# A hybrid decoder trunk: stick-breaking values scaled inside the attention's first unit, the gate block's subtractions side by side, the first group's transposes one step later, one quick pair fewer

## The chip, the core and the metric

The kernel runs on one core of a Trainium2 chip. The core has five engines that work side by side, each through its own queue in order: TensorE (PE in the profile, with its weight loads as PEld), VectorE (DVE), ScalarE (ACT), GpSimd (POOL) and SyncE (SP), which issues the DMAs. The metric is the time of one launch on the device, in microseconds (us); lower is better.

## The reference

Two layers work on 256 tokens of width 2048, all in float32. Each layer is:

```python
h = rms_norm(x, attn_norm)
g_q, g_k, g_v, g_gate, g_lr, s_q, s_k, s_v = split(h @ w_in)
log_a = log_sigmoid(g_lr @ w_gate_up + b_gate) / 16
o_gla = rms_norm(gla_chunked(g_q, g_k, g_v, log_a)) * silu(g_gate)   # 8 heads, chunks of 64
o_sb  = rms_norm(stick_breaking(rms_norm(s_q), rms_norm(s_k), s_v))  # 8 heads of 128
x = x + concat(o_gla, o_sb) @ w_o
x = x + square(relu(rms_norm(x, mlp_norm) @ w_up)) @ w_down          # 8192 hidden
```

Inside a chunk the gated linear attention works with `exp(b)`, `exp(-b)` and `exp(b_end - b)`, where `b` is the running sum of `log_a`. The stick-breaking attention weighs a key by `exp(log sigmoid(z) + suffix)`, where `suffix` is the sum of `log sigmoid(-z)` over the later keys before the query. It is computed as a product with a triangular matrix.

## The kernel before

**Products in parts.** The float32 operands of a large product are split into a high part, in a format that PE takes in one pass, and a low part, the rest; a product is three matmuls (high x high, high x low, low x high). The activations are split once. The weights are split while they stream in: SP loads a raw tile, ACT copies it into a high part `whi`, DVE subtracts to give the low part `wlo`. So every weight costs PE, ACT and DVE time, and the three engines work in a pipeline.

**Two ways to order the work.** Most of the time lies in `listed()`. It writes down all pieces of a long stretch (PE products in a fixed order, ACT and DVE pieces with lengths and dependences) and lets `Plan.run()` order ACT and DVE by due times, counted backwards from the PE pieces that need them. A first list (`front`) makes the three head blocks of layer 0: stick-breaking keys "sk", values "sv" and gated values "gv". A second one, per layer, makes the gate block, the output projection, the MLP and the three head blocks of the next layer. Each block goes over eight pairs of 128-row tiles. A pair in the table `QUICK` (or `FAST`, `QUICK_OUT`) is done in seven products of half-size blocks in place of eight, at the price of sums on DVE (line 821) and four weight parts in place of two. Lines 984 and 988 make the parts here, line 1078 is the matmul. The weight parts go round a ring of `RING = 5` slots: slot 0 is the list's own, slots 1 to 4 are the four `whi`/`wlo` tiles that are shared with the stretch in between.

**The attention stretch** lies between the lists and is written as a plain program, which the framework then orders by when it thinks things are ready. It is a chain of units of PE work:

- `ua`: the gate's low-rank columns and a quarter of the stick-breaking queries (272 columns, 8 steps). Lines 592 and 593 make its parts, 609, 612 and 615 are its matmuls.
- `ub`: the next quarter of the queries (256 columns, 8 steps).
- `uq`: the second half of the queries (512 columns, 8 steps).
- four units of `unit_t` (4 steps each, lines 634 and 638): the gated queries and keys.

After each step `tick()` is called. Other work hangs on the steps: `after(n, fn)` runs `fn` n steps later, and its ACT and DVE instructions queue behind the newest weight part on these engines. `sb_heads` does a group of four stick-breaking heads in two pairs: scores (`sb_scores`), three steps later the weights (`sb_weights`, whose exponentials are lines 757 and 758), one step later the outputs and their norm, and `last` steps later `to_operand`, which transposes the result on PE (line 788) and splits it (lines 793 and 794). `sb_qk` scales and norms the queries (lines 659 to 664) and turns them on PE (line 699). `gates(b)`, twice per layer, makes the three exponentials for the gated keys and queries. `row_of` spreads the row of inverse norms by two transposes (line 569) of a tile that POOL writes (line 568). Small PE results go through four PSUM banks in turn (`ps_tile`), so a tile waits for the readers of the fourth tile before it.

**The values.** `vs["sv", c]` holds half of the stick-breaking values, unscaled. `values()` multiplies them by the tokens' inverse norm on ACT (line 800, four instructions per layer) into tiles `v4`. In the kernel before this stands ahead of `ua`. The gated values are scaled inside the list (line 1543).

Of the kernel before, what the change touches and what calls it, by code (L numbers as in the profile page):

```python
# [13 lines left out]
AF = mybir.ActivationFunctionType  # L14
ALU = mybir.AluOpType
AX = mybir.AxisListType

P = 128
# [5 lines left out]
NT = T // P  # L24
# [5 lines left out]
CHUNK = 64  # L30
RANK = 16
GATE_TAU = 16.0
# [119 lines left out]
def trunk_kernel(  # L152
# [17 lines left out]
    nc = tc.nc  # L170
# [4 lines left out]
    def nm(s):  # L175
        uid[0] += 1
        return f"{s}_{uid[0]}"
# [15 lines left out]
    def open_scope(space, **want):  # L193
        close_scope(space)
        es = scopes[space] = ExitStack()
        for key, bufs in want.items():
            pools[key] = es.enter_context(
                tc.tile_pool(name=nm(key), bufs=bufs, reuse_waits="tile")
            )
# [14 lines left out]
    def ps_tile():  # L214
        turn_of["ps"] += 1
        return bank_tile(4 + (turn_of["ps"] - 1) % 4, "ps")
# [10 lines left out]
    def tmp(tag, shape, dt=F32, bufs=2):  # L227
        pool = pools["att"] if tag in ATT else pools["mlp"] if tag in MLP else tpool
        return pool.tile(list(shape), dt, tag=tag, name=nm(tag), bufs=bufs)
# [16 lines left out]
    dec = cpool.tile([P, 4], F32, name="dec")  # L246
# [110 lines left out]
    def after(n, fn):  # L357
        held.append((clock[0] + n, fn))
# [37 lines left out]
    class Operand:  # L396
# [19 lines left out]
    HEAD_KINDS = ("sk", "sv", "gv")  # L416
    QUICK = (
        ((5, 6), (5, 6, 7), (5, 6, 7), (5, 6)),
        ((4, 5, 6), (4, 5, 6), (4, 5, 6), (5, 6)),
    )  # L420
    HEADS = (
        ((0, 2, 1, 3, 5, 6, 4, 7), (4, 0, 5, 1, 6, 7, 3, 2), (4, 0, 5, 1, 6, 7, 3, 2), (4, 2, 1, 6, 5, 3, 7, 0)),
# [375 lines left out]
    def values(acc, v):  # L798
        for tt in range(NT):
            nc.scalar.activation(  # L800
                v[:, tt, :], acc[tt], AF.Copy, scale=st["rst"][:, tt : tt + 1]
            )
        return v
# [911 lines left out]
    kTs, vs = listed(0, True)  # L1715

    for l in range(DEPTH):
        wl = w_in[l]
        mixed = Operand()
        nxt = {}  # L1720

        open_scope("sbuf", att=1)
        if l == 0:
            load_small()
            build_constants()
            after(1, finish_small)
        else:
            layer_constants()
            load_gate_up(l)
        hT = st["hT"]  # L1730
        for c in range(2):
            vs[c] = values([vs["sv", c]()[:, tt, :] for tt in range(NT)], tmp("v4", [P, NT, 512], bufs=2))

        def sb_heads(g, qT, kT, v, first, last):

            state = {}

            def scores(hp):
                state[hp] = sb_scores(qT, kT, 2 * hp)
                after(3, lambda: weights(hp))  # L1740

            def weights(hp):
                state[hp] = sb_weights(*state[hp])
                after(1, lambda: outs(hp))

            def outs(hp):
                po = ps_tile()
                for j in range(2):
                    sb_out(po, j, state[hp], v, 2 * hp + j)
                o = norm_pair(po)  # L1750
                after(last, lambda: to_operand(mixed, 4 + 2 * g + hp, o, gain("so", l)))

            for hp in range(2):
                after(first[hp], lambda hp=hp: scores(hp))


        rst = st["rst"]
        turn_of["acc"] = 0
        ua = unit(hT, wl, 0, C_LR, RANK + 2 * P)
        lr = tmp("lr", [P, NT, RANK], bufs=1)  # L1760
        for tt in range(NT):
            nc.vector.tensor_scalar(
                lr[:, tt, :], ua[tt][:, :RANK], rst[:, tt : tt + 1], None, ALU.mult
            )
        qT = act_tile(F32)
        sb_qk(ua, RANK, 2, 0, rst, gqk[:, l : l + 1], qT, 5)


        gt = {}

        def gate_rows():
            lrT = tmp("lrT", [RANK + 1, T], bufs=1)
            nc.gpsimd.memset(lrT, 1.0)
            plr = ps_tile()
            for tt in range(NT):
                nc.tensor.transpose(plr[:RANK, tt * P : (tt + 1) * P], lr[:, tt, :], ident)
            nc.vector.tensor_copy(lrT[:RANK, :], plr[:RANK, :T])
            gt["row"] = row_of(rst)
            gt["lrT"] = lrT

        def gates(b):
            if b == 0:
                gt["e"] = [act_tile(F32) for _ in range(3)]
            eb, enb, ekd = gt["e"]
            pl = ps_tile()
            for e in range(2):
                ee = 2 * b + e
                nc.tensor.matmul(
                    pl[:, e * T : (e + 1) * T], lc["wg"][:, ee * P : (ee + 1) * P], gt["lrT"],
                    start=(e == 0), stop=True, skip_group_check=True,  # L1790
                )
            a = tmp("t2", [P, 512], bufs=4)
            nc.scalar.activation(a, pl, AF.Abs)
            nc.scalar.activation(a, a, AF.Exp, scale=-1.0)
            nc.scalar.activation(a, a, AF.Ln, bias=1.0)
            nc.vector.scalar_tensor_tensor(a, pl, 0.0, a, ALU.min, ALU.subtract)
            bc = tmp("t2", [P, 512], bufs=4)
            for e in range(2):
                es = slice(e * T, (e + 1) * T)
                nc.vector.tensor_tensor_scan(  # L1800
                    bc[:, es], lc["reset"], a[:, es], 0.0, ALU.mult, ALU.add
                )
            bs = slice(2 * b, 2 * b + 2)

            def fl(t):
                return t[:, bs, :].rearrange("p e t -> p (e t)")

            def chunks(t):
                return t.rearrange("p (n c) -> p n c", c=P)

            def heads(t):
                return t.rearrange("p (e t) -> p e t", t=T)

            nc.scalar.activation(
                dec[:, bs], heads(bc)[:, :, P + CHUNK - 1], AF.Exp, scale=1.0 / GATE_TAU
            )
            nc.vector.tensor_tensor(
                chunks(a), chunks(bc),
                chunks(bc)[:, :, CHUNK - 1 : CHUNK].to_broadcast([P, 4, P]), ALU.subtract,
            )  # L1820
            nc.scalar.activation(fl(eb), a, AF.Exp, scale=1.0 / GATE_TAU)
            nc.scalar.activation(fl(enb), a, AF.Exp, scale=-1.0 / GATE_TAU)
            nc.vector.tensor_tensor(
                heads(bc)[:, :, :P], heads(a)[:, :, P - 1 : P].to_broadcast([P, 2, P]),
                heads(a)[:, :, :P], ALU.subtract,
            )
            nc.scalar.activation(
                ekd[:, bs, :P], heads(bc)[:, :, :P], AF.Exp, scale=1.0 / GATE_TAU
            )
            rb = gt["row"].unsqueeze(1)  # L1830
            for t, w in ((eb, T), (enb, T), (ekd, P)):
                nc.gpsimd.tensor_tensor(
                    t[:, bs, :w], t[:, bs, :w], rb[:, :, :w].to_broadcast([P, 2, w]), ALU.mult
                )

        after(1, gate_rows)
        ub = unit(hT, wl, 0, C_SQ + 2 * P, 2 * P)
        sb_qk(ub, 0, 2, 2, rst, gqk[:, l : l + 1], qT, 3)
        sb_heads(0, qT, kTs[0], vs[0], (2, 6), 3)
        for b in range(2):  # L1840
            after(3 + 4 * b, lambda b=b: gates(b))


        uq = unit(hT, wl, 0, C_SQ + 512, 512)
        qT = act_tile(F32)
        sb_qk(uq, 0, 4, 0, rst, gqk[:, l : l + 1], qT, 3)
        sb_heads(1, qT, kTs[1], vs[1], (4, 7), 3)


        eb, enb, ekd = gt["e"]  # L1850
        qz = []
        for b in range(2):
            t = join(unit_t(hT, wl, C_GQ + b * 256))
            z = act_tile(F32, (P, 2, 2, T))
            nc.gpsimd.memset(z[0:DK, :, 1, :], 0.0)
            nc.gpsimd.memset(z[DK:P, :, 0, :], 0.0)
            for half in range(2):
                ps = slice(half * DK, (half + 1) * DK)
                nc.vector.scalar_tensor_tensor(
                    z[ps, :, half, :], t[ps], DK ** -0.5,  # L1860
                    eb[ps, 2 * b : 2 * b + 2, :], ALU.mult, ALU.mult,
                )
            qz.append(z)
        ke, kd = act_tile(F32), act_tile(F32)
        t = join(unit_t(hT, wl, C_GK))
        nc.vector.tensor_tensor(ke[:, :2, :], t, enb[:, :2, :], ALU.mult)
        nc.vector.tensor_tensor(kd[:, :2, :P], t[:, :, :P], ekd[:, :2, :P], ALU.mult)
        acc = unit_t(hT, wl, C_GK + 256)

        assert not held  # L1870

        open_scope("sbuf", mlp=1)
        kTs, vs = listed(l, False, mixed, vs, (ke, kd, qz, acc, enb, ekd))
# [40 lines left out]
```

## Time and profile before

| what | us |
|---|---|
| median of 3 runs (lowest, highest) | 2144.35 (2144.24, 2144.56) |
| the profiled execution | 2144.82 |
| its span, first to last instruction | 2143.0 |
| PE busy in it | 2130.7 |
| DVE busy | 1940.5 |
| ACT busy | 1424.3 |

The mean granted clock of TensorE is 0.998. The attention stretch begins at about 141 us in layer 0 and 1203 us in layer 1, and ends at about 256 and 1322 us; the lists fill the rest. In the rows below, a timeline row gives start, length, engine, line, operation and operands, and in brackets the idle time of the engine just before, with what ended it. A busy PE overlaps neighbouring matmuls, so its pace is read from the starts of its rows.

### The profile page before, as it was taken

The page shows a single profiled execution, that of the slowest core. Times are in us where ns is not written, and L with a number is a line of the kernel's source. Part 1 is how long each engine was busy: PE and PEld are TensorE (multiplying, and loading weights), DVE is VectorE, ACT ScalarE, POOL GpSimd, SP SyncE. Part 2 cuts the span into 40 slices and gives each one's busy share as a digit, 9 for nine tenths or more (in the row PEclk, how much of TensorE's full clock was granted, in tenths as well). Part 3 has the DMA queues.
Part 4 walks back from the last instruction along what each step waited for, and adds up shares of the span by engine and source line. Part 5 has one row for each costly group of instructions (what it writes and reads, how often), then busy time and mean ns, then how long its engine had stood idle before and what let it go on. Part 6 is the DMA issues. An engine that isn't in the chain of part 4 may idle for free. (4 is left out here: it accounts for less than half of the span.)

```text
span 2143.0 us, 27198 instructions
## 1 busy us (share of the span) xinstructions
PE 2130.7 (99%) x10111; PEld 1777.5 (83%) x10111; DVE 1940.5 (91%) x2408; ACT 1424.3 (66%) x2103; POOL 30.8 (1%) x57
## 2 busy tenths in 40 slices
PE   9999999999999999999999999999999999999999
PEld 7888888888888888888888888888888888888887
DVE  7977689999999899899999676899999999998997
ACT  7667677666576567577666585876765665765674
POOL 0001000000000000000000010000000000000000
PEclk9999999999999999999999999999999999999999
DMA  7645555555556456555665544555555655564564
GB/s 256 214 147 173 177 178 184 197 211 184 207 199 213 177 200 221 189 198 195 216 217 197 159 154 162 197 179 219 192 199 194 215 178 213 187 227 178 197 209 145
DMA packets 131448, 415.26 MB, mean 194 GB/s; under 512 B 6794, under 2 KB 31954, under 8 KB 131316
## 3 DMA queue, kind: packets, MB, share of 16 engines
q1 hardware_dynamic: 131316, 413.53, 55.8%
q8 instruction: 79, 1.29, 0.2%
q14 instruction: 53, 0.43, 0.1%
HBM read 409.31 MB, written 4.19 MB: 193 GB/s over the span
## 5 line engine op out<-in xcount | busy, mean ns | idle before, releaser
L984 ACT ACTIVATE whi<-raw 128x1024 fp32r<-128x1024 f32 (+1 forms) x706 | 733.7, 1055 | 383.0 <-issue 25.4
L988 DVE TENSOR_TENSOR wlo<-raw,whi 128x1024 fp32r<-128x1024 f32 (+1 forms) x706 | 844.1, 1217 | 25.6 <-ACT whi L984 16.9
L984 ACT ACTIVATE whi<-ts 128x1024 fp32r<-128x1024 f32 x139 | 147.0, 1058 | 113.5 <-PE m__1104_5064 L1078 6.5
L988 DVE TENSOR_TENSOR wlo<-ts,whi 128x1024 fp32r<-128x1024 f32 x139 | 170.0, 1223 | 48.6 <-ACT whi L984 48.4
L821 DVE TENSOR_TENSOR ts<-raw 128x1024 f32<-128x1024 f32 x139 | 169.5, 1220 | 0.6
L593 DVE TENSOR_TENSOR wlo<-raw,whi 128x1024 fp32r<-128x1024 f32 (+2 forms) x80 | 83.2, 1044 | 34.7 <-ACT whi L592 31.2
L984 ACT ACTIVATE whi<-t 128x512 fp32r<-128x512 f32 x139 | 86.8, 624 | 41.8 <-DVE t L821 12.6
L988 DVE TENSOR_TENSOR wlo<-t,whi 128x512 fp32r<-128x512 f32 x139 | 95.3, 686 | 10.0 <-ACT whi L984 9.9
L592 ACT ACTIVATE whi<-raw 128x1024 fp32r<-128x1024 f32 (+2 forms) x80 | 71.1, 890 | 48.3 <-PE acc L615 25.4
L821 DVE TENSOR_TENSOR t<-raw 128x512 f32<-128x512 f32 x139 | 95.4, 686 | 1.3
L821 DVE TENSOR_TENSOR raw<-ts,raw 128x512 f32<-128x512 f32 x139 | 95.2, 685 | 0.4
L634 PE MATMUL acc<-act,whi 128*128 128x512 f32 x256 | 92.1, 400 | 0.0
L638 PE MATMUL acc<-act,wlo 128*128 128x256 f32 x256 | 72.1, 281 | 0.0
L1212 ACT ACTIVATE act<-act,st 128x512 f32<-128x512 f32 x64 | 44.4, 717 | 32.7 <-DVE act L821 32.7
L609 PE MATMUL acc<-whi,act 128*128 128x272 f32 (+2 forms) x192 | 63.4, 331 | 1.4 <-ACT whi L592 1.4
L612 PE MATMUL acc<-wlo,act 128*128 128x272 f32 (+2 forms) x192 | 62.3, 325 | 0.2 <-DVE wlo L593 0.2
L615 PE MATMUL acc<-whi,act 128*128 128x272 f32 (+2 forms) x192 | 62.1, 324 | 0.0
L634 PEld LDWEIGHTS acc<-act,whi 128*128 128x128 f32 x256 | 48.2, 188 | 10.4
L638 PEld LDWEIGHTS acc<-act,wlo 128*128 128x128 f32 x256 | 48.3, 189 | 0.1
L492 DVE TENSOR_TENSOR act<-act,act 128x512 fp32r<-128x512 f32 x64 | 42.5, 685 | 0.0
L609 PEld LDWEIGHTS acc<-whi,act 128*128 128x128 f32 x192 | 37.0, 193 | 5.2 <-ACT whi L592 2.3
L488 ACT ACTIVATE act<-act 128x512 fp32r<-128x512 f32 x64 | 39.0, 622 | 0.5
(2819 smaller groups left out, 5775.7 us busy)
## 6 DMA issues: line engine op xcount, KB each, us to landing
raw<-in_w_up_dram SPq DMA_DIRECT2D x128, 1024.0 KB, 4.9
raw<-in_w_down_dram SPq DMA_DIRECT2D x128, 1024.0 KB, 5.3
raw<-in_w_in_dram SPq DMA_DIRECT2D x87, 1024.0 KB, 5.4
raw<-in_w_o_dram SPq DMA_DIRECT2D x32, 1024.0 KB, 5.2
raw<-in_w_in_dram SPq DMA_DIRECT2D x8, 544.0 KB, 3.8
raw<-in_w_in_dram SPq DMA_DIRECT2D x8, 512.0 KB, 3.8
act<-in_x_dram SPq DMA_DIRECT2D x7, 512.0 KB, 7.5
xs<-act SPq DMA_DIRECT2D x4, 512.0 KB, 3.0
```

Source lines behind the costliest of these rows:

```text
L492: nc.vector.tensor_tensor(lo, src, f32(h), ALU.subtract)
L592: newest["hi"] = nc.scalar.activation(hi[:, :, :width], r, AF.Copy).ins
L593: newest["lo"] = nc.vector.tensor_tensor(lo[:, :, :width], r, f32(hi[:, :, :width]), ALU.subtract).ins
L609: nc.tensor.matmul(o, xh[:, sl], whi[:, j, :width], start=(k == 0), stop=False)
L612: nc.tensor.matmul(o, xh[:, sl], wlo[:, j, :width], start=False, stop=False)
L615: nc.tensor.matmul(o, xl[:, sl], whi[:, j, :width], start=False, stop=(k == KT - 1))
L634: nc.tensor.matmul(acc[f], whi[:, j, sl], op.both(k), start=(k == 0), stop=False, skip_group_check=True,)
L638: nc.tensor.matmul(acc[f][:, T:], wlo[:, j, sl], xh, start=False, stop=(k == KT - 1), skip_group_check=True,)
L821: nc.vector.tensor_tensor(dst, a, b, op)
L984: nc.scalar.activation(box["h"][:, :n], src(), AF.Copy)
L988: nc.vector.tensor_tensor(box["l"][:, :n], src(), f32(box["h"][:, :n]), ALU.subtract)
L1212: nc.scalar.activation(box[h][:, tt, :], box[h][:, tt, :], AF.Relu, scale=rr[:, tt : tt + 1],)
```

## The change

Four edits, all in one diff:

- In layer 1's table, pair 4 leaves the quick pairs of the third head block (the gated values).
- `values()` for the stick-breaking values isn't called ahead of `ua` but after its steps 2 and 4, one half each.
- In `gates(b)` the two subtractions follow each other on DVE, and the small exponential `dec` comes behind them. The second subtraction reads the running sum `bc` in place of the shifted `a` (the same difference) and writes a temporary of its own, `ends`, in place of `bc`.
- `last` of the first group's `sb_heads` is 4 in place of 3.

```diff
     QUICK = (
         ((5, 6), (5, 6, 7), (5, 6, 7), (5, 6)),
-        ((4, 5, 6), (4, 5, 6), (4, 5, 6), (5, 6)),
+        ((4, 5, 6), (4, 5, 6), (5, 6), (5, 6)),
     )
...
+        def scaled_values(c):
+            vs[c] = values([vs["sv", c]()[:, tt, :] for tt in range(NT)], tmp("v4", [P, NT, 512], bufs=2))
+
         for c in range(2):
-            vs[c] = values([vs["sv", c]()[:, tt, :] for tt in range(NT)], tmp("v4", [P, NT, 512], bufs=2))
+            after(2 + 2 * c, lambda c=c: scaled_values(c))
...
-            nc.scalar.activation(
-                dec[:, bs], heads(bc)[:, :, P + CHUNK - 1], AF.Exp, scale=1.0 / GATE_TAU
-            )
+            ends = tmp("t2", [P, 2, P], bufs=4)
             nc.vector.tensor_tensor(
                 chunks(a), chunks(bc),
                 chunks(bc)[:, :, CHUNK - 1 : CHUNK].to_broadcast([P, 4, P]), ALU.subtract,
             )
+            nc.vector.tensor_tensor(
+                ends, heads(bc)[:, :, P - 1 : P].to_broadcast([P, 2, P]),
+                heads(bc)[:, :, :P], ALU.subtract,
+            )
+            nc.scalar.activation(
+                dec[:, bs], heads(bc)[:, :, P + CHUNK - 1], AF.Exp, scale=1.0 / GATE_TAU
+            )
             nc.scalar.activation(fl(eb), a, AF.Exp, scale=1.0 / GATE_TAU)
             nc.scalar.activation(fl(enb), a, AF.Exp, scale=-1.0 / GATE_TAU)
-            nc.vector.tensor_tensor(
-                heads(bc)[:, :, :P], heads(a)[:, :, P - 1 : P].to_broadcast([P, 2, P]),
-                heads(a)[:, :, :P], ALU.subtract,
-            )
-            nc.scalar.activation(
-                ekd[:, bs, :P], heads(bc)[:, :, :P], AF.Exp, scale=1.0 / GATE_TAU
-            )
+            nc.scalar.activation(ekd[:, bs, :P], ends, AF.Exp, scale=1.0 / GATE_TAU)
...
-        sb_heads(0, qT, kTs[0], vs[0], (2, 6), 3)
+        sb_heads(0, qT, kTs[0], vs[0], (2, 6), 4)
```

## The prediction

> **What bounds the kernel now.** I read the page first, for which engine fills the span.
>
> ```profile
> span 2143.0 us, 27198 instructions
> PE 2130.7 (99%) x10111; PEld 1777.5 (83%) x10111; DVE 1940.5 (91%) x2408; ACT 1424.3 (66%) x2103; POOL 30.8 (1%) x57
> ```
>
> TensorE (PE) is busy for all but 12.3 us. So no edit that merely relieves VectorE (DVE) or ScalarE (ACT) can pay; a gain must be a PE wait that goes, or slow PE time. The second view is the waits of PE; the third, stretches with the granted clock (columns: length; busy time of PE, weight load, DVE, ACT, POOL; PE clock; DMA).
>
> ```profile
> PE ps L788 <- ACT hA L757: 3.0, 2, 1.5
> ...
> PE acc L609 <- ACT whi L592: 1.4, 1, 1.4
> ...
> PE ps L569 <- POOL bc L568: 0.4, 1, 0.4
> PE acc L612 <- DVE wlo L593: 0.2, 1, 0.2
> ```
>
> ```profile
> 142.00:149.00 7.00, 7.00 (x56) 6.80 (x55) 3.63 (x9) 4.70 (x9) 0.38 (x2) 1.00 0.36 113
> 1206.00:1211.00 5.00, 4.76 (x26) 4.62 (x25) 1.05 (x2) 0.69 (x2) 0.00 (x0) 0.66 0.39 108
> 199.00:213.00 14.00, 12.49 (x81) 10.89 (x80) 10.85 (x19) 11.14 (x39) 5.66 (x7) 1.00 0.49 147
> 256.00:1203.00 947.00, 947.00 (x4338) 784.84 (x4337) 890.93 (x1079) 629.83 (x867) 3.49 (x9) 1.00 0.57 198
> ```
>
> Two places lose time. One is the first group's transposes (L788), once per layer, 1.5 us each. The other is the start of layer 1's attention: 1.4 + 0.4 + 0.2 us of waits, and behind them 5 us at a clock of 0.66. The long listing between (256 to 1203) has no PE gap at all.
>
> The fourth view, the PE timeline, gives both layers' first unit, from its first matmul (in layer 1 from the transposes ahead of it) to that of the next unit (256 columns):
>
> ```profile
> 140.88 0.28 PE L609 MATMUL acc<-whi,act 128*128 128x272 f32 x1
> ...
> 153.28 0.28 PE L609 MATMUL acc<-whi,act 128*128 128x256 f32 x1
> ...
> 1203.17 0.27 PE L569 MATMUL ps<-ident,bc 128*128 128x128 f32 x1
> 1203.85 0.33 PE L569 MATMUL ps<-ident,bc 128*128 128x128 f32 x1 [0.41 <-POOL bc L568]
> 1205.62 0.52 PE L609 MATMUL acc<-whi,act 128*128 128x272 f32 x2 [1.44 <-ACT whi L592]
> ...
> 1219.79 0.28 PE L609 MATMUL acc<-whi,act 128*128 128x256 f32 x1
> ```
>
> The same unit takes 153.28 - 140.88 = 12.40 us in layer 0 and 1219.79 - 1203.17 = 16.62 in layer 1. It is 4.2 us dearer there: waits of 2.1, and (1 - 0.66) x 5 = 1.7 of slow clock.
>
> **Why layer 1 starts late.** The ACT timeline of both starts:
>
> ```profile
> 138.42 0.66 ACT L592 ACTIVATE whi<-raw 128x544 fp32r<-128x544 f32 x1
> ...
> 141.10 1.32 ACT L800 ACTIVATE v<-act,st 128x512 f32<-128x512 f32 x2
> ...
> 1192.57 0.65 ACT L592 ACTIVATE whi<-raw 128x544 fp32r<-128x544 f32 x1
> ...
> 1197.92 0.66 ACT L592 ACTIVATE whi<-raw 128x544 fp32r<-128x544 f32 x1 [1.98 <-PE m__2295_10486 L1078]
> 1200.01 0.72 ACT L1543 ACTIVATE act<-act,st 128x512 f32<-128x512 f32 x1 [1.43 <-DVE act L821]
> ...
> 1203.70 0.71 ACT L800 ACTIVATE v<-act,st 128x512 f32<-128x512 f32 x1
> 1204.32 0.71 ACT L1543 ACTIVATE act<-act,st 128x512 f32<-128x512 f32 x1
> 1204.93 0.64 ACT L592 ACTIVATE whi<-raw 128x544 fp32r<-128x544 f32 x1
> ```
>
> In layer 0 four high parts of the first unit are made before PE gets there (the fourth at 138.42). In layer 1 three are, and the one PE waits for ends at 1205.57. The code says which: the listing puts part i in slot i mod 5, of which 1 to 4 are the attention's four buffers and 0 is its own; a quick pair makes 4 parts, a plain one 2. By the tables the listing before layer 1 makes 20 + 40 + 190 + 176 + 66 = 492 parts, numbered from 5, so its last is 496, slot 1: the buffer that the next unit's **first** part needs. That part can't be begun until the last matmul of the listing is over (1203.17), and then sits behind L800 (1203.70) and L1543 (1204.32). The front listing ends on number 70, slot 0, and layer 0 has no such wait.
>
> **The change, part by part.**
>
> *Pair 4 of layer 1's last head block becomes plain.* Its price, from this block's own PE timeline: a quick pair from 1167.12, a plain one from 1171.88, the next from 1177.32.
>
> ```profile
> 1167.12 0.39 PE L1078 MATMUL m__2285_10450<-whi,act 128*128 128x512 f32 x1
> ...
> 1171.88 0.39 PE L1078 MATMUL m__2285_10450<-whi,act 128*128 128x512 f32 x1
> ...
> 1177.32 0.39 PE L1078 MATMUL m__2285_10450<-whi,act 128*128 128x512 f32 x1
> ```
>
> Quick 4.76 us, plain 5.44: **+0.7 us** of PE, on the path, certain. The DVE and ACT work it saves (the sums and two parts) is hidden and worth nothing. But the listing then ends on 494, slot 4: the first unit's part 0 gets the buffer of 491, free three parts earlier (3 x 2.7 us, half a plain pair each), and only part 3 has to wait for the end, 4.5 us before PE wants it (a part is 12 of the unit's 96 matmuls, 1.5 us).
>
> *Values scaled at steps 2 and 4 of the unit.* Four ACT instructions of 0.7 us move behind the high parts 1 and 3; nothing is added. Queued behind them on ACT are the later high parts, which have three buffers (4.5 us) of lead against 1.3 us per pair of values. Their first reader is 20 steps on. In layer 0 they already run at 141.10, when the four first parts are made; no gain there.
>
> Together these two take away layer 1's late start: 4.2 us by the comparison with layer 0, of which 0.2 comes back with the two L569 transposes, which layer 0 pays in its second unit. I take **-4.0**, between -2.3 (the waits and little else) and -4.2. By the Trainium skill, page "TensorE: Matmul & The Clock Gate", section "Why this matters for your kernels", only PE-idle gaps above about 3 us drop the clock. By that rule the slow 5 us would not go with gaps this short, and the gain would be about 2.5; but the clock of 0.66 follows directly on these gaps, so I let the rows decide.
>
> *Transposes one step later.* Layer 0's place, on PE, ACT and DVE:
>
> ```profile
> 200.99 0.40 PE L634 MATMUL acc<-act,whi 128*128 128x512 f32 x1
> ...
> 201.34 0.40 PE L634 MATMUL acc<-act,whi 128*128 128x512 f32 x1
> 203.25 0.66 PE L788 MATMUL ps<-ident,on 128*128 128x128 f32 x4 [1.51 <-ACT hA L757]
> ```
>
> ```profile
> 202.29 0.42 ACT L1827 ACTIVATE act<-t 128x256 f32<-128x256 f32 x1 [1.12 <-DVE t L1823]
> 202.62 0.58 ACT L757 ACTIVATE hA<-ps 128x512 f32<-128x512 f32 x1
> 203.09 0.38 ACT L758 ACTIVATE hA<-ps 128x256 f32<-128x256 f32 x1
> ```
>
> ```profile
> 199.01 0.69 DVE L1817 TENSOR_TENSOR t<-t 128x512 f32<-128x512 f32 x1
> ...
> 200.75 1.51 DVE L1823 TENSOR_TENSOR t<-t 128x256 f32<-128x256 f32 x1
> ...
> 1224.93 0.42 DVE L664 TENSOR_TENSOR act<-act,st 128x256 f32<-128x256 f32 x1
> ```
>
> The transposes write the PSUM bank that held the second head pair's scores; the exponential L757 must have read it. L757 stands in ACT's queue behind the gate's L1827, which waits for the gate's second subtraction L1823. From 201.34 to 203.25 is 1.91 us for a matmul that takes 0.23: 1.7 us lost. One step later PE has the rest of part 1 (three more pairs of matmuls, 0.35 each as from 200.99 to 201.34) in front, so it comes at about 202.75 and not 201.57. Bank order doesn't change: at the later steps nothing else takes a bank ahead of these two.
>
> *Subtractions in one run.* L1823 then follows L1817 at 199.6 and not L593, and ends at 201.1 if it still takes 1.51, at 200.0 if it takes the 0.42 us of L664, an operation of this size; its form (a broadcast first operand) is kept, so 1.51. Either way L757 ends by about 202.1 and not 203.2, ahead of the transposes. The low part L593 that stood between them goes 1.5 us later; it is made three parts ahead of PE (eight pairs of 0.35, so 2.8 us, each), which covers that. Alone on the path: nothing. A third temporary per gate block comes out of a ring of four whose older users are done: nothing.
>
> The wait should go in both layers: 2 x 1.7 = 3.4. What is late next are the second group's turns, whose norm runs through the same loaded ACT (11.14 of 14 us busy):
>
> ```profile
> 209.07 1.29 DVE L664 TENSOR_TENSOR act<-act,st 128x512 f32<-128x512 f32 x2
> ```
>
> ```profile
> 209.82 0.33 PE L699 MATMUL ps<-ident,act 128*128 128x128 f32 x1
> ```
>
> PE would come 1.7 us sooner, at 208.1; the norm, freed by 1.1 us, has its first half at about 208.6. I leave 0.25 us per layer for it: **-2.9**, between -1.2 (L757 no earlier, so PE waits from 202.75 to 203.25, and 0.6 at the turns) and -3.4.
>
> **Sum:** -4.0 - 2.9 + 0.7 = -6.2 us. The profiled execution took 2144.82 (span 2143.0 and 1.8 around it), so 2138.6; from the median 2144.35, which is 0.5 lower, **2138.2 us**. With all bounds at their better end -6.9 (2137.4), at their worse end -2.8 (2141.5).
>
> **Rivals.**
> 1. *The step only passes the wait on*: the second group's turns wait for the norm in place of L788, if ACT's queue doesn't come forward. The norm's first half is then ready at 209.7 (half of L664's 1.29 after 209.07), and of the 1.7 us 1.6 are lost again. For: ACT at 80% there. Against: L1827's idle 1.12 us goes. Third term -0.2: -4.0 - 0.2 + 0.7 = -3.5, 2140.9.
> 2. *Layer 1's start stays late in part*: the parts come, but values or gv scalings (four L1543, 2.8 us) still stand ahead of one, a wait of about 1 us stays and the clock falls all the same. Then the first term is about 4.0 - 1.0 - 1.7 = -1.3: -1.3 - 2.9 + 0.7 = -3.5, 2140.9 again. Against: layer 0, with both kinds of work, shows none. If the table's edit doesn't shift the buffers as I count, it is this case too.
> 3. *Slower*: the listing's DVE and ACT order is planned backwards from its end. A quick pair has a sum of this group,
>
> ```profile
> L821 DVE TENSOR_TENSOR ts<-raw 128x1024 f32<-128x1024 f32 x139 | 169.5, 1220 | 0.6
> ```
>
> its low part at the same 1.2, and three operations of half the size at 0.7. So 4.5 us less DVE work in the last block (139 quick pairs become 138) moves the due times of all before it. DVE is 891 of 947 us busy. If in each of the four quarters of the MLP one sum now comes behind a low part and PE waits as at 1203 (2.1 and 1.7 of clock), that is 4 x 3.8 = 15.2: +9.0, 2153.4. It decides from two such stalls up. Against: those 947 us have no PE gap, and the change only takes DVE work away.
>
> **Chances:** forecast 0.70, rival 1 0.12, rival 2 0.11, rival 3 0.07. What this kernel's measurement can tell from no change is 0.2%, 4.3 us, so faster means below 2140.1. Forecast nearly always (0.67) and the better half of rivals 1 and 2 (0.06): faster 0.73; the rest of these 0.20: same; slower 0.07. Range 2136.6 to 2142.0: the bounds, with some room below for waits I can't see.
>
> **What would show it.** In the changed profile: L788's wait gone from PE's list; no wait on L592 at layer 1's start and a clock of 1.00 there; first unit near 12.4 us; quick pairs' sums (L821 into ts) 138 times; the listing before layer 1 0.7 us longer and the rest of it unchanged. Wrong if L699, L765 or L1078 appear with waits over 0.5 us, or the listing is longer by more than that.

## The result

The changed kernel takes 2138.98 us (median of 9 runs, 2138.61 to 2140.13), against 2144.56 for the kernel before on the same chips. The ratio is 0.9974, with a 95% interval of 0.9963 to 0.9984: 5.6 us or 0.26% faster. The forecast was 2138.2, 6.2 us less than before. Beside the experiments below, one launch of the kernel before took 8014.98 us; it is in no comparison.

The page of the kernel after, with the rows that answer those of before:

```profile
span 2137.1 us, 27196 instructions
...
PE 2128.5 (100%) x10114; PEld 1776.4 (83%) x10114; DVE 1930.0 (90%) x2403; ACT 1422.7 (67%) x2101; POOL 31.5 (1%) x57
...
L821 DVE TENSOR_TENSOR ts<-raw 128x1024 f32<-128x1024 f32 x138 | 168.3, 1219 | 0.6
```

138 quick pairs are left of 139, and the record has three matmuls more on PE. The waits of PE no longer hold L788, L569, L609 or L612. One row is new:

```profile
PE ps L699 <- DVE act L664: 1.3, 2, 0.7
```

These are the second group's turns, twice, 0.7 us each. That is the wait that the prediction named as the next one, but larger. By the prediction's own last line a wait over 0.5 us on L699 is a sign that it is wrong, and this sign is here.

The start of layer 1, on PE (the first unit's first matmul and that of the second unit) and on ACT, and the stretch with its clock (columns as in the prediction, and GB/s at the end):

```profile
1202.44 0.28 PE L609 MATMUL acc<-whi,act 128*128 128x272 f32 x1
...
1214.47 0.28 PE L609 MATMUL acc<-whi,act 128*128 128x256 f32 x1
```

```profile
1194.48 0.66 ACT L592 ACTIVATE whi<-raw 128x544 fp32r<-128x544 f32 x1 [4.38 <-PE m__2291_10466 L1078]
...
1202.70 0.66 ACT L592 ACTIVATE whi<-raw 128x544 fp32r<-128x544 f32 x1
1203.26 0.71 ACT L800 ACTIVATE v<-act,st 128x512 f32<-128x512 f32 x1
```

```profile
1202.00:1209.00 7.00, 7.00 (x56) 6.92 (x55) 3.60 (x5) 5.39 (x9) 0.00 (x0) 1.00 0.32 86
```

The first high part is made at 1194.48, eight us ahead of its use. The last of the first four begins at 1202.70, right after the last matmul of the list (1202.21). PE goes on without a gap at full clock: the unit takes 12.03 us.

The place of the first group's transposes in layer 0, on PE, ACT and DVE:

```profile
202.47 0.60 PE L788 MATMUL ps<-ident,on 128*128 128x128 f32 x4
...
209.18 0.33 PE L699 MATMUL ps<-ident,act 128*128 128x128 f32 x1 [0.66 <-DVE act L664]
```

```profile
201.69 0.57 ACT L757 ACTIVATE hA<-ps 128x512 f32<-128x512 f32 x1
```

```profile
199.32 0.42 DVE L1822 TENSOR_TENSOR t<-t 128x256 f32<-128x256 f32 x1
...
208.44 1.29 DVE L664 TENSOR_TENSOR act<-act,st 128x512 f32<-128x512 f32 x2
```

The transposes don't wait. The second subtraction (now L1822) takes 0.42 us, where it took 1.51. PE then stands before L699 until the norm's first half is done.

From the starts of PE's rows in every profile the time can be split by stage. Where two kernels have a stage in common, its length repeats within 0.1 us (the first column apart), far better than the whole time does, so the experiments below are read from them. The list before layer 1 ends, and layer 1's first unit begins, with PE's first row behind the list. Where that unit takes longer than 12.03 us the two L569 transposes lie in it, otherwise in the second unit:

| kernel | until the first unit | list before layer 1 | first unit, layer 1 | second unit, layer 1 | four gated units, layers 0 / 1 | list of layer 1 | span |
|---|---|---|---|---|---|---|---|
| before | 140.88 | 947.38 | 16.62 | 12.15 | 59.58 / 59.60 | 821.19 | 2143.03 |
| after | 140.59 | 948.01 | 12.03 | 12.63 | 58.51 / 58.53 | 821.17 | 2137.10 |
| table alone | 140.40 | 948.01 | 12.03 | 12.63 | 59.59 / 59.54 | 821.18 | 2139.02 |
| values alone | 141.75 | 947.31 | 13.88 | 12.14 | 59.61 / 59.59 | 821.19 | 2141.09 |
| step alone | 141.85 | 947.31 | 16.62 | 12.13 | 59.39 / 59.38 | 821.18 | 2143.48 |
| gate block alone | 141.64 | 947.31 | 15.10 | 12.14 | 58.09 / 58.09 | 821.19 | 2139.18 |
| before, rows on DVE | 141.88 | 947.34 | 15.10 | 12.13 | 58.43 / 58.45 | 821.19 | 2140.14 |
| after without the step | 140.63 | 948.01 | 12.03 | 12.63 | 58.10 / 58.10 | 821.18 | 2136.32 |
| after, second group later | 140.85 | 948.20 | 12.03 | 12.63 | 57.74 / 57.74 | 821.40 | 2136.22 |
| after, ring shifted | 142.03 | 947.34 | 12.03 | 12.63 | 58.65 / 58.55 | 821.38 | 2138.24 |
| ring shifted, second group later | 140.92 | 947.54 | 12.03 | 12.63 | 57.74 / 57.74 | 821.60 | 2135.83 |
| second group later, no step | 141.00 | 948.29 | 12.03 | 12.63 | 57.99 / 57.99 | 821.38 | 2136.95 |
| after, once more | 141.65 | 948.05 | 12.03 | 12.63 | 58.51 / 58.51 | 821.17 | 2138.19 |

What isn't in the table (layer 0's first and second unit, the third of both layers) is 12.4, 12.6 and 30.3 in each. The kernel after against before: -4.59 + 0.48 at layer 1's start, -2.14 in the gated units, +0.63 in the list, and -0.29 at the very start, which no edit touches. The sum is -5.9.

Five of these kernels were run once only: the step alone (2145.30 us), the gate block alone (2141.00), the rows on DVE (2141.92), the second group later (2137.93) and the same without the step (2138.66). A single whole time can be off by the 1.1 us between two forms of the launch's start (last section), so they are judged by their stages.

### The profile page after: what moved, and what is told of

Same layout as the page of the kernel before. It is cut to its first block, busy times and chain, and to the rows that moved or that the text cites. A ratio compares the mean times of both kernels' runs of the same rounds, so it can differ in the third digit from the quotient of the medians.

```text
span 2137.1 us, 27196 instructions
## 1 busy us (share of the span) xinstructions
PE 2128.5 (100%) x10114; PEld 1776.4 (83%) x10114; DVE 1930.0 (90%) x2403; ACT 1422.7 (67%) x2101; POOL 31.5 (1%) x57
## 4 chain that ended last, share of the span: by engine, by line
PE 97%; issue 1%; DVE 1%; ACT 1%; DMA 0%; POOL 0%; POOLq 0%
PE acc L634 2%; PE acc L609 1%; PE acc L638 1%; PE acc L612 1%; PE acc L615 1%; PE m__38_167 L1078 1%; PE m__40_173 L1078 0%; PE m__2636_12050 L1078 0%; PE m__596_2644 L1078 0%; PE m__691_3115 L1078 0%; PE m__2731_12521 L1078 0%; PE m__602_2669 L1078 0%; PE m__2642_12075 L1078 0%; PE m__50_207 L1078 0%; PE m__2641_12066 L1078 0%
## 5 line engine op out<-in xcount | busy, mean ns | idle before, releaser
L593 DVE TENSOR_TENSOR wlo<-raw,whi 128x1024 fp32r<-128x1024 f32 (+2 forms) x80 | 81.3, 1017 | 38.9 <-ACT whi L592 38.2
L984 ACT ACTIVATE whi<-t 128x512 fp32r<-128x512 f32 x138 | 86.2, 625 | 41.7 <-DVE t L821 12.6
L609 PE MATMUL acc<-whi,act 128*128 128x272 f32 (+2 forms) x192 | 62.8, 327 | 0.0
L612 PE MATMUL acc<-wlo,act 128*128 128x272 f32 (+2 forms) x192 | 61.5, 320 | 0.0
L609 PEld LDWEIGHTS acc<-whi,act 128*128 128x128 f32 x192 | 36.4, 190 | 3.6 <-issue 0.7
```

Of the source, the lines that this page charges most:

```text
L593: newest["lo"] = nc.vector.tensor_tensor(lo[:, :, :width], r, f32(hi[:, :, :width]), ALU.subtract).ins
L609: nc.tensor.matmul(o, xh[:, sl], whi[:, j, :width], start=(k == 0), stop=False)
L612: nc.tensor.matmul(o, xh[:, sl], wlo[:, j, :width], start=False, stop=False)
L984: nc.scalar.activation(box["h"][:, :n], src(), AF.Copy)
```

## Experiments

### Layer 1's start: the table or the values?

The table's edit alone:

```diff
-        ((4, 5, 6), (4, 5, 6), (4, 5, 6), (5, 6)),
+        ((4, 5, 6), (4, 5, 6), (5, 6), (5, 6)),
```

> Only the table's edit (pair 4 of layer 1's third head block plain), everything else as before. Buffer theory: PE waits at layer 1's start because the first unit's part 0 needs the buffer of the listing's very last part, and this edit alone frees it three parts earlier. Then the first unit of layer 1 takes about 12.0 to 12.3 us (16.6 before), its wait on L592 and the low clock are gone, the listing is 0.6 us longer, and the whole is 3.5 us faster, near 2141. Rival, ACT's queue: the four value scalings ahead of the unit are what makes the part late; then a wait of about 1 us stays here, the clock falls behind it, the unit takes 14 to 16 us, and the whole is within 2 us of before.

2141.25 us, ratio 0.9984 (0.9974 to 0.9994). The first unit takes 12.03 us, as in the kernel after, and none of its waits is left. The list is 0.63 longer. ACT at the start of layer 1 in this kernel, and the unit's stretch:

```profile
1203.60 0.66 ACT L592 ACTIVATE whi<-raw 128x544 fp32r<-128x544 f32 x1
1204.26 0.73 ACT L1543 ACTIVATE act<-act,st 128x512 f32<-128x512 f32 x1
```

```profile
1203.34:1215.37 12.03, 12.03 (x98) 12.03 (x96) 6.35 (x10) 6.17 (x10) 0.00 (x0) 1.00 0.50 135
```

So the buffer is the cause. The scalings of the values stand nowhere in the way here; the last of the four begins over ten us ahead of the unit:

```profile
1192.74 0.71 ACT L800 ACTIVATE v<-act,st 128x512 f32<-128x512 f32 x1
```

The values alone:

```diff
+        def scaled_values(c):
+            vs[c] = values([vs["sv", c]()[:, tt, :] for tt in range(NT)], tmp("v4", [P, NT, 512], bufs=2))
+
         for c in range(2):
-            vs[c] = values([vs["sv", c]()[:, tt, :] for tt in range(NT)], tmp("v4", [P, NT, 512], bufs=2))
+            after(2 + 2 * c, lambda c=c: scaled_values(c))
```

> Only the value scalings moved into the first unit's steps 2 and 4, everything else as before. Buffer theory: part 0 still can't be begun before the listing's last matmul is over, but it no longer stands behind the scalings; its high part is ready about 1.3 us sooner, so of the 2.1 us of waits about 0.8 to 1 stay, the first unit of layer 1 takes 13 to 15.5 us, depending on whether the clock still falls. Rival, ACT's queue: no wait, 12.0 us, 4 us faster in all. Layer 0's first unit: 12.4 us by both.

2142.51 us, ratio 0.9988 (0.9979 to 0.9997); first unit 13.88. PE's waits around it:

```profile
PE ps L569 <- POOL bc L568: 0.4, 1, 0.4
PE acc L612 <- DVE wlo L593: 0.2, 1, 0.2
PE acc L609 <- ACT whi L592: 0.2, 1, 0.2
```

The wait for the high part shrinks from 1.4 to 0.2 us, the three waits together from 2.1 to 0.8, as expected, and the clock doesn't fall. So the scalings did make the wait longer, but the wait doesn't go with them, and beside the table's edit this one adds nothing (12.03 with and without it).

The counter-test is the kernel after with pair 4 quick again, and with it all the list's VectorE work; only the ring is turned by one buffer for layer 1:

```diff
-        ((4, 5, 6), (4, 5, 6), (5, 6), (5, 6)),
+        ((4, 5, 6), (4, 5, 6), (4, 5, 6), (5, 6)),
...
+        part_turn[0] += l
         turn_of["acc"] = 0
```

> The kernel after with the table's edit undone (pair 4 of layer 1's third head block quick again) and, in its place, the first unit of layer 1 starting one buffer further round the ring (the turn of the parts raised by one ahead of it). Buffer theory: no wait at layer 1's start, first unit about 12.0 us, and the listing is 0.6 us shorter than after, so the whole is 0.6 us faster than the kernel after. Rival, VectorE's load: the table's edit helps because 4.5 us of VectorE work go; then the start waits again: 13.5 to 16.6 us.

The first unit takes 12.03 us again and the list 947.34. So it is the place in the ring and not the load on VectorE. (The values' move is in this kernel too; the ring turned without it was not run.) As a whole it was 2139.62 us (ratio 0.9975, 0.9965 to 0.9984), not the expected gain on the kernel after: of the 0.67 us that the list gains, 0.16 goes in the gated units and 0.21 in layer 1's list, which leaves 0.3, and this profile began 1.4 us late for a reason of its own (below).

### The gated units: the step or the gate block?

The step alone:

```diff
-        sb_heads(0, qT, kTs[0], vs[0], (2, 6), 3)
+        sb_heads(0, qT, kTs[0], vs[0], (2, 6), 4)
```

> Only the first group's transposes one step later. The exponential L757 still ends late (behind L1827 and the gate's slow subtraction), so the transposes still wait about 0.5 us, and the rest of the gain is lost at the second group's turns (L699), whose norm is no earlier: the four gated units take 59.3 us per layer (59.6 before, 58.5 with all edits), the whole is 0.3 to 0.8 us faster. Rival: the step alone takes the wait away for good, 58.2 us per layer, 2.8 us faster in all.

59.39 and 59.38: 0.2 us per layer, nearly as expected. The wait is passed on:

```profile
PE ps L699 <- DVE act L664: 1.8, 2, 0.9
...
PE ps L788 <- ACT hA L757: 0.7, 2, 0.3
```

The single run took 2145.3 us, no gain that can be seen.

The gate block alone, on the kernel before (some of the lines that it adds; the whole of its edit is in the section on the change):

```diff
...
+            nc.vector.tensor_tensor(
+                ends, heads(bc)[:, :, P - 1 : P].to_broadcast([P, 2, P]),
+                heads(bc)[:, :, :P], ALU.subtract,
+            )
+            nc.scalar.activation(
+                dec[:, bs], heads(bc)[:, :, P + CHUNK - 1], AF.Exp, scale=1.0 / GATE_TAU
+            )
...
```

> Only the gate block's subtractions in one run. The second subtraction takes 0.42 us as in the kernel after and L1827 no longer holds ACT up; L757 ends about 0.7 us earlier, the transposes still come right behind the scores and wait 0.8 to 1.1 us in place of 1.5: the four gated units take 59.0 to 59.2 us per layer, the whole is about 1 us faster. Rival: the edit is off the path and changes nothing (59.6). Second rival: it takes the whole wait away (58.2).

58.09 in both layers: 1.5 us less per layer. The expectation (59.0 to 59.2) missed; it is the second rival (58.2) that came, and the kernel is **0.4 us per layer better than the kernel after**, which has the step as well. On PE and DVE:

```profile
203.37 0.66 PE L788 MATMUL ps<-ident,on 128*128 128x128 f32 x4 [0.16 <-ACT hA L757]
...
209.82 0.33 PE L699 MATMUL ps<-ident,act 128*128 128x128 f32 x1
```

```profile
209.08 1.29 DVE L664 TENSOR_TENSOR act<-act,st 128x512 f32<-128x512 f32 x2
```

The transposes hardly wait for L757, and L699 comes without a wait. The gated units begin at 196.97 here and at 195.92 in the kernel after; counted from there the norm L664 begins at 12.11 here and 12.52 there. So with the step the norm is 0.4 us later. In both profiles a weight part's L593 stands just ahead of it on DVE, and that is what comes later; that the step's new place among ACT's and DVE's work does this is read from the order of the rows and was not tested by itself.

So I took the step back out of the kernel after:

```diff
-        sb_heads(0, qT, kTs[0], vs[0], (2, 6), 4)
+        sb_heads(0, qT, kTs[0], vs[0], (2, 6), 3)
```

> The kernel after with the transposes back at three steps; the table, the values and the gate block stay changed. If the gate block's edit did the work and the extra step only moved PE's wait to the second group's turns, the four gated units take 58.1 us per layer (58.5 after, 59.6 before) and the whole is 0.8 us faster than the kernel after: near 2138.1 in a profiled run with a span near 2136.3. Rival: with layer 1's start mended too the order falls differently, and the transposes wait again: 59.0 or more.

58.10 / 58.10, span 2136.32, 2138.02 us (ratio 0.9969, 0.9957 to 0.9980). Of L788's wait this is left:

```profile
PE ps L788 <- ACT hA L757: 0.3, 2, 0.2
```

Beside this, the kernel after with the step has 58.51. The gate block's edit does all of the work here; the step costs 0.4 us per layer.

### Why the subtraction was slow

The kernel before, with the gate block's three multiplications after the exponentials moved from GpSimd to VectorE, one step later:

```diff
-            for t, w in ((eb, T), (enb, T), (ekd, P)):
-                nc.gpsimd.tensor_tensor(
-                    t[:, bs, :w], t[:, bs, :w], rb[:, :, :w].to_broadcast([P, 2, w]), ALU.mult
-                )
+            def rows():
+                for t, w in ((eb, T), (enb, T), (ekd, P)):
+                    nc.vector.tensor_tensor(
+                        t[:, bs, :w], t[:, bs, :w], rb[:, :, :w].to_broadcast([P, 2, w]), ALU.mult
+                    )
+
+            after(1, rows)
```

> The kernel before, but the three multiplications by the row of inverse norms that follow each gate block's exponentials are made by VectorE one step later, and not by GpSimd at once; the second subtraction keeps its place, its operands and its broadcast. Sharing theory: that subtraction takes 1.52 us before only because GpSimd's multiplications begin 0.3 us ahead of it; without them it takes 0.42 us. Rival: its operands make it slow; it stays at 1.52. Its time as a whole says little, since VectorE gets 4 x 1.8 us more work.

The subtraction of before, at its old place with its old operands (durations in ns, smallest, median, largest):

```profile
L1823 DVE TENSOR_TENSOR t<-t x4: 417/419/419, 184.3 to 1265.0; 128x256 f32<-128x256 f32 x4
```

0.42 us, where all four took 1.51 to 1.52 in the kernel before. So its operands were never the matter. GpSimd's multiplications in the kernel before and in the kernel after:

```profile
200.44 3.63 POOL L1832 TENSOR_TENSOR act<-act,row 128x512 f32<-128x512 f32 x3 [12.76 <-ACT act L1821]
```

```profile
200.15 3.81 POOL L1834 TENSOR_TENSOR act<-act,row 128x512 f32<-128x512 f32 x3 [12.63 <-ACT act L1829]
```

Before, L1823 began at 200.75, 0.3 us behind the first of these. One of GpSimd's large multiplications takes 1.50 in the mean there, so the first was over at about 201.9 (an estimate), and the subtraction ended 0.3 us later, at 202.26: as if it had waited, and then taken its 0.42. After, L1822 is over at 199.74, ahead of GpSimd's start. The Trainium skill, page "GPSIMD Engine Reference", section "Specifications", says that GpSimd's access to SBUF is shared with VectorE, with contention for VectorE instructions with two SBUF inputs. The trace agrees, and not for the subtraction alone. In layer 0's first gate block of the kernel before, GpSimd's three multiplications run from 183.02 to 187.68, and the low part behind the subtraction, with two SBUF inputs as well, is slow too:

```profile
184.78 2.32 DVE L593 TENSOR_TENSOR wlo<-raw,whi 128x1024 fp32r<-128x1024 f32 x1
```

Its usual length is 1.22. In the kernel after no L593 takes over 1.25, but there GpSimd's four large multiplications of layer 0 take 1.82 in the mean in place of 1.50. So the delay has not gone: it has moved to GpSimd, on which PE doesn't wait in these stages.

This kernel gains 1.15 us per layer in the gated units, though VectorE has more to do: the same wait of ACT behind the subtraction, made shorter in another way.

### What is left: the turns' wait

The kernel after with the second group one step later:

```diff
-        sb_qk(uq, 0, 4, 0, rst, gqk[:, l : l + 1], qT, 3)
-        sb_heads(1, qT, kTs[1], vs[1], (4, 7), 3)
+        sb_qk(uq, 0, 4, 0, rst, gqk[:, l : l + 1], qT, 4)
+        sb_heads(1, qT, kTs[1], vs[1], (5, 8), 3)
```

> The kernel after with the second group (turns, scores and all that follows) one step later. If the turns wait for their norm (L664), and for nothing else, the 0.8 us wait on L699 is gone and the four gated units take about 57.7 us per layer in place of 58.5. Rival: the wait goes on to the scores or to the end of the stretch, where the last transposes now come one step before the list: 58.1 to 59.

57.74 in both layers, and PE has no wait at all behind its first 100 us. So behind the wait for the norm no other one stood. 0.2 us per layer come back in the lists that follow (948.20 and 821.40), so the net gain on the kernel after is 1.1; the single run took 2137.93.

Without the step, and with the second group later:

```diff
-        sb_heads(0, qT, kTs[0], vs[0], (2, 6), 4)
+        sb_heads(0, qT, kTs[0], vs[0], (2, 6), 3)
...
-        sb_qk(uq, 0, 4, 0, rst, gqk[:, l : l + 1], qT, 3)
-        sb_heads(1, qT, kTs[1], vs[1], (4, 7), 3)
+        sb_qk(uq, 0, 4, 0, rst, gqk[:, l : l + 1], qT, 4)
+        sb_heads(1, qT, kTs[1], vs[1], (5, 8), 3)
```

> The kernel after with the second group one step later and the first group's transposes back at three steps. If the extra step is worth something once the turns give way, the four gated units take 0.3 us more per layer here than with it (57.7), from the short wait for L757; if the norm's chain on ScalarE and VectorE takes that in, the same 57.7.

57.99: once the turns give way, the step is worth 0.25 us per layer. In these runs it pays only with this partner.

The two findings together, ring shifted in place of the plain pair and the second group later, again on the kernel after:

```diff
-        ((4, 5, 6), (4, 5, 6), (5, 6), (5, 6)),
+        ((4, 5, 6), (4, 5, 6), (4, 5, 6), (5, 6)),
...
+        part_turn[0] += l
         turn_of["acc"] = 0
...
-        sb_qk(uq, 0, 4, 0, rst, gqk[:, l : l + 1], qT, 3)
-        sb_heads(1, qT, kTs[1], vs[1], (4, 7), 3)
+        sb_qk(uq, 0, 4, 0, rst, gqk[:, l : l + 1], qT, 4)
+        sb_heads(1, qT, kTs[1], vs[1], (5, 8), 3)
```

> The kernel after with both findings: one buffer further round the ring in layer 1 in place of the plain pair, and the second group one step later. The two act at different places, so the gains add: listing near 947.4 us (948.0 after), four gated units 57.7 us per layer (58.5 after), first unit of layer 1 12.0: 2.1 us faster than the kernel after in runs with the same start, and about 0.35% faster than before. Rival: they disturb each other (a later unit meets another buffer), and less than 1.5 us comes.

2137.45 us (2137.05 to 2138.37), ratio to before 0.9966 (0.9954 to 0.9978), against 2139.25 for the kernel after on the same chip. By stages it is 1.6 us shorter than the kernel after (-0.47 in the list, -1.56 in the gated units, +0.43 in layer 1's list), and not 2.1. It is the quickest kernel of these experiments.

The kernel after beside it, with no edit at all:

> The kernel after itself once more, beside the others on the same chip. 2138.6 to 2140.2; where a run is 1.3 to 1.5 us above the others, its first units of the front begin later (at 142 us and not 140.6), since PE's clock stays low longer at the very start; by stages all else is the same.

2138.63 to 2140.16. All its stages agree with the first profile within 0.04 us but one: the first unit begins at 141.65 and not 140.59.

## Why the prediction was right, and where it wasn't

- **Layer 1's start**, forecast -4.0: -4.1 (first unit -4.59, second +0.48, of which I had 0.2). The reading of the ring holds: the table's edit alone gives all of it, and so does turning the ring. I put the values' move on the same account; it adds nothing there. What the sum took as safe is not quite so: the slow clock behind the waits, 1.5 us of the 4.1, is absent in two kernels with the same waits (last section). The forecast let the rows of the kernel before decide, and for that kernel they were right.
- **The plain pair**, forecast +0.7: +0.63.
- **Gated units**, forecast -2.9: -2.14. This is the term that was mis-sized, by two steps. The first is the 0.25 us per layer left for the second group's turns. The prediction's own times, PE at 208.1 and the norm's first half at 208.6, give 0.5, and the kernel with the second group later shows 0.77 per layer (58.51 to 57.74). That the turns' norm is the next wait in line was right.
- **Which edit pays** is the second, and here the mechanism was wrong in part. The chain (PE waits for L757, ACT's queue for the second subtraction) was right. But the gain was put down to the step, and the gate block's edit alone was priced at nothing. Measured it is the reverse: the gate block alone takes 1.5 us per layer, and the step on top of it costs 0.4. The prediction's own figure, L757 done by 202.1 in place of 203.2, already took 1.1 us off a wait of 1.7 without the step. That the term came out as near as it did is luck in so far as both edits were made together.
- **The subtraction**: I took 1.51 us, because the new form keeps the broadcast first operand. It takes 0.42. It was GpSimd beside it; the row with GpSimd's busy time was quoted, but not followed up.
- **Rival 1** (the step only passes the wait on) is what the step does by itself: 0.2 us for both layers was its price, 0.4 was measured. **Rival 2** (a part still late at layer 1's start) left no trace: the unit has no wait.
- **The transposes' place**, 202.75, isn't what the working beside it gives (201.57 and three pairs of 0.35 make 202.6). In the kernel after they begin 6.55 us into the gated units, which would be 202.76 there, so nothing hangs on it.
- **The values in layer 0**: no gain, as said (12.40 in both).
- **Rival 3**, a new plan that stalls the list: nothing of it, the list is longer by the plain pair alone.
- The -0.3 us at the very start was not foreseen and belongs to no edit.

## What to carry to other kernels

Where two stretches share a ring of buffers, count on which slot the first one ends; one buffer of offset cost 2.6 to 4.1 us here, and shifting the ring cured it without giving up work, though part of the gain went again in later stages. The wait in ACT's in-order queue was cured better at the instruction that held the queue (0.42 in place of 1.51 us on VectorE) than by moving the reader later, which passed the wait on until the next reader was moved as well. An instruction that is far slower than others of its size is worth a look at what runs beside it. And stage lengths read from the trace settle what whole times with a spread of 1.5 us can't.

## What the runs showed of the hardware

The slow clock behind a wait is not a fixed price. The step-alone and gate-alone kernels have the same three waits at layer 1's start (0.4, 1.4 and 0.2 us); their clocks behind them, first step alone, then gate alone:

```profile
1207.00:1212.00 5.00, 4.90 (x27) 4.91 (x28) 0.77 (x2) 1.19 (x2) 0.00 (x0) 0.66 0.40 108
```

```profile
1205.00:1210.00 5.00, 4.76 (x37) 4.54 (x38) 1.92 (x3) 1.32 (x2) 0.00 (x0) 1.00 0.40 108
```

With the slow clock the unit takes 16.62 us, without it 15.10, and the kernel with the rows on VectorE has 15.10 too. Why the clock falls in one and not in the other, these runs don't show. The Trainium skill, page "TensorE: Matmul & The Clock Gate", section "What's actually happening", describes the window over which PE's work is watched: it lasts 3.4 us, runs freely and isn't reset when a kernel starts. If it matters where in such a window a gap falls, equal waits can come out either way; no run here shows the window.

Chance from launch to launch is hardly the whole of it. A launch of the kernel before that kept its clock would take about 1.5 us less. Of 47 launches beside the experiments 46 took 2144.1 to 2145.9 us, and one 2143.46. Nor has any of the 47 a mean granted clock of 1.000, which all seven launches of the kernel after above 2139.5 us have. So in the kernel before the clock seems to fall nearly always, and one profile each of the two kernels that kept it is all there is.

The very start of the launch has two forms as well. In the kernel after (first) PE is back to its pace of 0.23 us per matmul at 12.1; in the same kernel once more (second) matmuls are 0.43 us apart until 13.3:

```profile
12.11 0.39 PE L1078 MATMUL m__40_173<-whi,act 128*128 128x512 f32 x1
12.34 0.60 PE L516 MATMUL m__46_193<-ident,act 128*128 128x128 f32 x4
```

```profile
12.47 0.63 PE L1078 MATMUL m__40_173<-wlo,act 128*128 128x512 f32 x1
12.90 0.62 PE L1078 MATMUL m__40_173<-whi,act 128*128 128x512 f32 x1
13.32 0.64 PE L516 MATMUL m__46_193<-ident,act 128*128 128x128 f32 x4
```

By the L516 row the second is 1.0 us behind, nearly all of the 1.1 us between the two profiles of one program. Profiles of the other kernels begin at 140.4 to 141.0 or at 141.6 to 142.0. The granted clock in the records shows it the wrong way round. Here is the stretch ahead of these rows, of the first and then of the second (start and end, length, busy time of PE, PEld, DVE, ACT and POOL, granted clock, DMA share, GB/s):

```profile
7.00:12.00 5.00, 4.37 (x11) 3.25 (x12) 2.97 (x6) 4.16 (x12) 0.00 (x0) 0.66 1.04 407
```

```profile
7.00:13.00 6.00, 5.33 (x12) 3.86 (x13) 3.31 (x6) 4.53 (x12) 0.00 (x0) 1.00 1.03 398
```

The second is given as 1.00 and the first as 0.66, and yet the second's matmuls (0.43 us from start to start) are as far apart as those of the first, and for longer.
